# Pacing the side work of a hybrid encoder layer: Fourier tables split once, two paces, one more high part

## The chip, the cores and the metric

The kernel runs on one core of one Trainium2 chip, in one launch. The metric is the device time of that launch in microseconds (us). Before the change it is 2509.24 us, the median of three runs (2506.54 to 2513.37).

## The reference

One layer over T = 2048 positions of 1024 channels (a batch of one), all in float32:

```python
h = rms_norm(x, norm_g)
z = h @ w_in                                   # 1024 x 10240 columns
a_val, qkv, c_in, d_in, br_gates, merge = split(z)
y_a = real(fft2(a_val in 4 groups of 128 channels, over (positions, channels)))
y_b = neighborhood_attention(q, k, v, rpb)     # 8 heads, 32 x 64 grid, 8 x 16 window
y_c = silu(layer_norm(depthwise_conv31(ga * sigmoid(gb))))
y_d = u * (w_s @ layer_norm(v) + b)            # per chunk of 128 positions
proj   = [ (y_n * silu(gate_n)) @ w_branch[n] for n in 4 branches ]     # 512 -> 1024
merged = sum(sigmoid(merge_n) * proj_n)
out    = rms_norm(x + merged @ w_out, final_g)
```

## The kernel before

Each float32 operand is split in two parts of a reduced matmul type: a high part, cast on ScalarE (`split`, L226), and a low part, the difference, on VectorE (L227). A product is three matmuls, high by high, high by low and low by high (`mm3`, L235 to L244). The positions are worked in two halves of 1024.

**The first phase** (here: z phase) computes z = h @ w_in in 20 blocks of 512 columns per half, in the order of `BLOCKS` (L32 to L37): mixers and gates first, and as the last eight, blocks 12 to 19, the merge gates m3, n3, m2, n2, m0, n0, m1, n1. A block is done as seven products after Strassen and Winograd (`ORDER`, L53), 168 matmuls of 128x512. The weights come in tiles `wq` on SyncE's queue (SP) and are split into `whi` and `wlo`, five in advance (`W_BUFS`).

**Sides.** What is not the large products is written as Python generators ("sides"), which `tick` (L172) advances between the matmuls. A tick follows 6 matmuls, so that a block has 28; at each tick a side gains as many steps as its rate says. A side that must have ended by a certain block is drained there: all of its remaining steps are emitted at once. The rates and the blocks thus set where each instruction is written in the program; Tile, which builds the program, then sets each engine's order with the written order as priority. Each engine runs its own list in that order and waits by semaphores. The sides of the second half in question are:

- `conv_norm` (L826): the layer norm of the convolution in five pieces of 208 positions: channel sums (POOL adds at L230, a matmul at L802, VectorE at L849, ScalarE squares at L852, a second sum), then a square root (L859), reciprocals (L867), products (L871), 20 Silu activations (L875) and the stores. Its rate is `NORM_RATE`. It is drained at block `F_AT` = 15.
- `fourier` (L1081), begun at the same block, in four channel groups. Each group loads 1 MB (`fa`), does the butterflies on VectorE (L1109 to L1162), splits the result into `XS` (L226, L227), and then in `sums` (L1177) does products with nine tables (48 matmuls of 256 columns) and with a cosine and a sine (18 of 384). The tables `t_fft` are loaded as `traw` and split into `tH` and `tL` anew in each group. One rate, `FFT_RATE`, goes for all of it. It is drained at block 19.

**The second phase** (y phase) goes, for each half, through the branches 3, 2, 0, 1 and then the output product. Per branch, `project` (L1384) runs 8 column tiles (`dt`) of four `mm3` each (`kt`) on the four parts `yH`, `yL`. These parts come from `gated` (L1368): a part's `yL` is loaded, cast into `yH` (one of `YH_BUFS` = 5 buffers) and subtracted. Branch 1 (attention) has a gate besides, loaded into the only buffer `bg` and multiplied on VectorE. `ahead` (L1299) places the next branch's parts: part 0 at dt 6, and parts 1, 2 and 3 at dt 7, behind kt 0, 2 and 3. The branch's four parts in use hold four of the five buffers.

Beside the y phase runs the side `attention` (L941) with 128 items of 128 queries each: scores on PE (L997) and a minimum on VectorE (L1003); exp (L1006) and a scaling (L1008) on ScalarE; `turn`, four transposes on PE (L1019) and a split (L1021, L1022); `apply`, the products with v (L1035, L1037). `ATT_TURN` = 2 is the number of scores by which an item's transposes stand behind its own scores, `SC_BUFS` = 4 the buffers for scores, and `ATT_RATE` = (1.45, 0.85) the steps per tick, the second number in the branch-1 block of half 0. `fetch` (L1292) emits what steps are missing there before it loads the attention's result as a part of branch 1.

Of the kernel before, what the change touches and what calls it, by code (L numbers as in the profile page):

```python
# [9 lines left out]
F32 = mybir.dt.float32  # L10
F32R = mybir.dt.float32r
BF16 = mybir.dt.bfloat16
# [5 lines left out]
P = 128  # L18
# [37 lines left out]
CTYPE = (0, 1, 1, 2)  # L56

CONV_RATE = (0.55, 0.72)
NORM_RATE = (1.3, 1.6)
MIX_RATE = 0.7  # L60
FFT_RATE = 2.1
ATT_RATE = (1.45, 0.85)

X_AT = 17
F_AT = 15

Z_BUFS = 3
ZS_BUFS = 4
W_BUFS = 5
YH_BUFS = 5  # L70
YL_BUFS = 6
YW_BUFS = 4
SG_BUFS = 2
SC_BUFS = 4
VT_BUFS = 4

ATT_LEAD = 8
ATT_TURN = 2
ATT_APPLY = 3
FFT_LEAD = 12  # L80
SUM_LEAD = 4
# [3 lines left out]
PRE_RATE = 0.24  # L85
# [78 lines left out]
class Trunk:  # L164
# [254 lines left out]
    def scratch(self):  # L419
        d = lambda n, s, t=F32: self.dp.tile(s, t, name=n, tag=n)  # L420
        self.qd = [d(f"qd{j}", [2, P, T], F32R) for j in range(4)]
        self.kd = [d(f"kd{j}", [2, P, T], F32R) for j in range(4)]

        self.vd = d("vd", [8, GW, 4, ROWS // 4, P], F32R)
        self.fd = d("fd", [P, 16, W])
        self.yd = [[d(f"yd{n}{c}", [P, T]) for c in range(4)] for n in range(4)]
        self.gd = [[d(f"gd{n}{c}", [P, T]) for c in range(4)] for n in range(3)]

        self.wbd = [[d(f"wb{n}{i}", [P, 2, 512], F32R) for i in range(KT)] for n in range(4)]
        self.wod = [[d(f"wo{u}{i}", [P, 2, 512], F32R) for i in range(KT)] for u in range(2)]  # L430
        self.md = [[[d(f"md{n}{c}{h}", [P, HALF]) for h in range(2)] for c in range(KT)] for n in range(4)]
# [89 lines left out]
    def z_phase(self, ctx):  # L521
# [25 lines left out]
        for i in range(4):  # L547
            self.w_load(0, i)
        self.x_load(0, range(4, 8))
        xl, mix, conv, fft, pre = (self.side(r) for r in (2.0, MIX_RATE, CONV_RATE[0], FFT_RATE, PRE_RATE))  # L550
        self.conv, self.glu = conv, {}
        self.conv_side = self.sides[2]
        ps = [(self.psz if k < 2 else self.psp)() for k in range(4)]
        for j in range(4):
            self.x_square(j)
# [526 lines left out]
    def fourier(self):  # L1082
        nc, pool = self.nc, self.fp
        for _ in range(FFT_LEAD):
            yield
        raw = self.zs().rearrange("p (a c) -> p a c", a=4)[:, 0:2]
        self.load(out=raw, in_=self.io["t_cs"].rearrange("p (a c) -> p a c", a=2))
        cH = pool.tile([P, 2, P], F32R, name="cH", tag="cH")
        cL = pool.tile([P, 2, P], F32R, name="cL", tag="cL")
        self.split(cH, cL, raw)  # L1090
        self.cH, self.cL = cH, cL
        for g in range(4):
            yield from self.butterflies(g)
            yield from self.sums(g, *self.fX)

    def butterflies(self, g):
# [72 lines left out]
    def sums(self, g, XH, XL):  # L1169
        nc, pool = self.nc, self.fp  # L1170
        tt = nc.vector.tensor_tensor
        A, S = ALU.add, ALU.subtract
        cH, cL = self.cH, self.cL
        yt = pool.tile([P, T], F32, name="yf", tag="f8", bufs=3)
        yv = yt.rearrange("p (k1 k2) -> p k2 k1", k2=16)

        raws, ahead = [], []  # L1177

        def table(k):
            if k < 9:  # L1180
                raw = pool.tile([P, 3 * P], F32, name="traw", tag="traw", bufs=2)
                self.load(out=raw, in_=self.io["t_fft"][:, k * 384:(k + 1) * 384])
                raws.append(raw)

        def parts(k):
            if k < 9:
                tH = pool.tile([P, 3 * P], F32R, name="tH", tag="tH", bufs=2)
                tL = pool.tile([P, 3 * P], F32R, name="tL", tag="tL", bufs=2)
                self.split(tH, tL, raws.pop(0))
                ahead.append((tH, tL))  # L1190
                table(k + 2)

        table(0)
        table(1)
# [3 lines left out]
        for k0, k9 in ((0, 3), (3, 6), (6, 9)):  # L1198
            n = k9 - k0

            fH = pool.tile([P, 2, 3, P], F32R, name="fH", tag="fH")
            fL = pool.tile([P, 2, 3, P], F32R, name="fL", tag="fL")
            for k in range(k0, k9):
                yield
                tH, tL = ahead.pop(0)
                parts(k + 1)
                yield
                o = self.psp()[:, 0:2 * P]
                cplx = 0 < k < 8
                self.mm3([o], (XH[:, k], XL[:, k]), [(tH[:, P:3 * P], tL[:, P:3 * P])], True, not cplx)  # L1210
                if cplx:
                    self.mm3([o], (XH[:, 8 + k], XL[:, 8 + k]), [(tH[:, 0:2 * P], tL[:, 0:2 * P])], False, True)
                src = o.rearrange("p (s c) -> p s c", s=2)
                fh = fH[:, :, k - k0]
                nc.scalar.copy(fh, src)
                tt(out=fL[:, :, k - k0], in0=src, in1=fh.bitcast(F32), op=S)
            for _ in range(3):
                yield

            pu, pv = self.psp()[:, :n * P], self.psp()[:, :n * P]  # L1220
            for o, i in ((pu, 0), (pv, 1)):
                self.mm3([o], (cH[:, i], cL[:, i]),
                         [tuple(f[:, i, 0:n].rearrange("p k c -> p (k c)") for f in (fH, fL))], True, True)
            vs = self.zs()
            nc.scalar.copy(vs[:, :n * P], pv)
            pu3 = pu.rearrange("p (k c) -> p k c", c=P)
            vs3 = vs[:, :n * P].rearrange("p (k c) -> p k c", c=P)
            tt(out=yv[:, k0:k9], in0=pu3, in1=vs3, op=S)
            lo, hi = max(k0, 1), min(k9, 8)
            if lo < hi:  # L1230

# [33 lines left out]
    def y_phase(self, ctx):  # L1265
# [18 lines left out]
        for bi, (half, n) in enumerate(blocks):  # L1284
# [15 lines left out]
            def ahead(dt, kt):  # L1300

                if following is None or bi % 4 == 3:
                    return
                if dt == 4 and kt < 2:
                    fetch(kt)
                elif dt == 6 and kt == 0:
                    self.gated(nxt, *following, 0)
                elif dt == 7:
                    if kt < 2:
                        fetch(kt + 2)  # L1310
                    self.gated(nxt, *following, (1, None, 2, 3)[kt])

            self.project(ys, mg, bi % 4 == 0, ahead)
            if bi == 0:
# [52 lines left out]

    def gated(self, ys, half, n, kt):  # L1368

        if kt is None:  # L1370
            return
# [70 lines left out]
    def finish(self, u, row, ss, ps, t0):  # L1442
        nc, pool = self.nc, self.bp
        o = row[u]
        self.tt(o, ps, o, ALU.add)
        junk = pool.tile([P, 512], BF16, name="junk", tag="junk", bufs=1)
        nc.scalar.activation(out=junk, in_=o, func=AF.Square, accum_out=ss[:, u:u + 1])
        self.tt(o, o, self.fgb[:, 512 * u:512 * u + 512], ALU.mult, None if u else nc.gpsimd)
        if u == 0:
# [25 lines left out]
```

## Time and profile before

| | |
|---|---|
| median of three runs | 2509.24 us |
| the profiled execution | 2512.59 us |
| its span, first to last instruction | 2510.8 us (1.8 us lie around it) |
| mean granted TensorE clock | 0.982 |
| PE busy | 2398.4 us, 96% |
| VectorE (DVE), ScalarE (ACT), POOL busy | 1711.0, 1221.4, 337.4 us |
| DMA | 516.23 MB, 206 GB/s over the span |
| blocks 12 to 19 of the second half, start to end | 1339.4 to 1722.0 us |
| y phase, half 0 / half 1 | 1723.6 to 2188.7 / 2188.7 to 2510.8 us |

PE is the engine that is nearly always busy. A microsecond in which PE stands idle in the midst of the span, or runs below its full clock, can be won; work on any other engine costs only where PE, or a store at the end, waits for it. In the second half, blocks 14 to 19 start at 1417.6, 1457.7, 1522.6, 1581.9, 1631.7 and 1683.8 us.

### The profile page before, as it was taken

What the parts mean: (1) busy time and instruction counts of PE and PEld (TensorE: products, weight loads), DVE (VectorE), ACT (ScalarE), POOL (GpSimd) and SP (SyncE); (2) the same over time, 40 slices, a digit from 0 to 9 for tenths busy, and PEclk for the clock granted to TensorE, in tenths of its full rate; (3) what the DMA queues carried; (4) which work ended last, traced back from release to release, by engine and by line L of the source; (5) the groups of instructions that cost most, each with busy time, mean ns of one, the idle gap of its engine ahead of it and who ended that gap; (6) DMA issues with size and microseconds to landing.
All of it is one profiled execution on the core that took longest, in us unless ns stands there. A gap on an engine that the chain in (4) does not pass through costs nothing.

```text
span 2510.8 us, 34022 instructions
## 1 busy us (share of the span) xinstructions
PE 2398.4 (96%) x11804; PEld 1999.8 (80%) x11804; DVE 1711.0 (68%) x2972; ACT 1221.4 (49%) x2282; POOL 337.4 (13%) x290
## 2 busy tenths in 40 slices
PE   7999999999999999999999978999999799999998
PEld 6998878878878899877878867887777588777786
DVE  7585799996565537479898367764677776565433
ACT  5343545544574534354544565543655646652012
POOL 1000000000221100000000220001244333312220
PEclk9999999999999999999999989999999899999999
DMA  4353766654565335376755456667899788876566
GB/s 162 127 157 137 258 220 224 221 178 168 180 240 185 118 119 150 130 234 212 243 185 167 140 183 204 222 213 242 259 275 274 223 268 264 290 270 226 208 234 216
DMA packets 251720, 516.23 MB, mean 206 GB/s; under 512 B 26006, under 2 KB 124054, under 8 KB 250908
## 3 DMA queue, kind: packets, MB, share of 16 engines
q1 hardware_dynamic: 197276, 442.73, 54.7%
q10 hardware_dynamic: 54272, 71.32, 8.0%
q8 instruction: 93, 1.52, 0.2%
q14 instruction: 79, 0.65, 0.1%
HBM read 346.18 MB, written 167.77 MB: 205 GB/s over the span
## 4 chain that ended last, share of the span: by engine, by line
PE 64%; DVE 17%; DMA 8%; ACT 5%; issue 5%; POOL 1%; SPq 0%; ACTq 0%; DVEq 0%; POOLq 0%
PE z L238 36%; PE b L238 17%; DVE acc L785 6%; PE p L238 3%; DVE wlo L227 2%; PE p L1019 2%; PE p L997 2%; DMA pw<-in_wb_dram 2%; PE p L1035 1%; PE p L503 1%; DMA pw<-in_wo_dram 1%; DVE wq L230 1%; ACT sc L1006 1%; DMA yd<-yf 1%; DVE zu L233 1%
## 5 line engine op out<-in xcount | busy, mean ns | idle before, releaser
L226 ACT CAST whi<-wq 128x512 fp32r<-128x512 f32 x560 | 347.0, 621 | 489.4 <-PE z L238 282.1
L227 DVE TENSOR_TENSOR wlo<-wq,whi 128x512 fp32r<-128x512 f32 x560 | 391.7, 702 | 263.8 <-ACT whi L226 254.1
L238 PE MATMUL z<-hH,whi 128*128 128x512 f32 x1088 | 428.1, 394 | 10.5 <-ACT whi L226 8.0
L238 PE MATMUL z<-hH,wlo 128*128 128x512 f32 x1088 | 425.3, 391 | 1.6 <-DVE wlo L227 1.6
L238 PE MATMUL z<-hL,whi 128*128 128x512 f32 x1088 | 424.8, 390 | 0.0
L238 PE MATMUL b<-hH,whi 128*128 128x512 f32 x816 | 323.7, 397 | 8.5 <-DVE zu L233 8.3
L238 PE MATMUL z<-yH,yw 128*128 128x512 f32 x1024 | 308.7, 404 | 17.1 <-ACT yH L226 12.8
L238 PE MATMUL b<-hH,wlo 128*128 128x512 f32 x816 | 320.1, 392 | 0.8 <-DVE wlo L227 0.8
L238 PE MATMUL b<-hL,whi 128*128 128x512 f32 x816 | 320.2, 392 | 0.0
L785 DVE SCALAR_TENSOR_TENSOR acc<-hb,cw,acc 128x1009 f32<-128x1009 f32 (+1 forms) x240 | 306.7, 1281 | 2.0 <-ACT acc L781 1.5
L238 PEld LDWEIGHTS z<-hH,whi 128*128 128x128 f32 x1088 | 205.2, 189 | 54.9 <-ACT whi L226 8.5
L238 PEld LDWEIGHTS z<-yH,yw 128*128 128x128 f32 x1024 | 192.9, 193 | 61.5 <-ACT yH L226 17.5
L238 PEld LDWEIGHTS z<-hH,wlo 128*128 128x128 f32 x1088 | 204.9, 188 | 45.5 <-DVE wlo L227 2.3
L238 PEld LDWEIGHTS z<-hL,whi 128*128 128x128 f32 x1088 | 205.1, 188 | 41.1
L984 POOL TENSOR_TENSOR e<-mask,gt 128x512 f32<-128x512 bf16 x96 | 133.0, 1414 | 448.4 <-DMA gt<-in_rp_dram 380.9
L238 PEld LDWEIGHTS b<-hH,whi 128*128 128x128 f32 x816 | 154.4, 189 | 45.1 <-DVE zu L233 11.4
L238 PEld LDWEIGHTS b<-hH,wlo 128*128 128x128 f32 x816 | 154.5, 189 | 33.2 <-DVE wlo L227 1.1
L238 PEld LDWEIGHTS b<-hL,whi 128*128 128x128 f32 x816 | 154.4, 189 | 29.8
L238 PE MATMUL z<-yL,yw 128*128 128x512 f32 x512 | 164.9, 399 | 2.8 <-DVE yL L227 2.8
L1006 ACT ACTIVATE sc<-sc,mn 128x512 f32<-128x512 f32 x128 | 92.1, 720 | 97.4 <-DVE mn L1003 97.2
L1022 DVE TENSOR_TENSOR pp<-p,pp 128x512 fp32r<-128x512 f32 x128 | 87.1, 685 | 55.6 <-ACT pp L1021 55.3
L238 PE MATMUL z<-yw,mH 128*128 128x512 f32 x384 | 121.3, 397 | 2.6 <-DMA yw<-wo 2.1
(232 smaller groups left out, 4195.6 us busy)
## 6 DMA issues: line engine op xcount, KB each, us to landing
wq<-in_wz_dram SPq DMA_DIRECT2D x140, 512.0 KB, 3.6
wk<-wq SPq DMA_DIRECT2D x80, 512.0 KB, 2.7
wq<-wk SPq DMA_DIRECT2D x80, 512.0 KB, 3.9
yw<-wb SPq DMA_DIRECT2D x64, 512.0 KB, 4.6
sg<-md SPq DMA_DIRECT2D x64, 512.0 KB, 4.9
yw<-wo SPq DMA_DIRECT2D x64, 512.0 KB, 4.3
vt<-vd SPq DMA_DIRECT2D x64, 320.0 KB, 7.3
md<-zs ACTq DMA_DIRECT2D x64, 256.0 KB, 3.3
```

The lines of the kernel that those rows point to most:

```text
L226: nc.scalar.copy(hi, src)
L227: (eng or nc.vector).tensor_tensor(out=lo, in0=src, in1=hi.bitcast(F32), op=ALU.subtract)
L230: (eng or self.nc.vector).tensor_tensor(out=out, in0=a, in1=b, op=op)
L233: self.nc.vector.tensor_tensor(out=out, in0=a, in1=b, op=ALU.add)
L238: mm = lambda *a, **kw: self.nc.tensor.matmul(*a, skip_group_check=chained, **kw)
L503: self.nc.tensor.transpose(ps[:, j * P:(j + 1) * P], self.x_parts(j, which)[:, k * P:(k + 1) * P], self.ident)
L785: nc.vector.scalar_tensor_tensor(out=a, in0=hb[:, j:j + n], scalar=self.cw[:, i, j:j + 1], in1=a, op0=ALU.mult, op1=ALU.add)
L984: nc.gpsimd.tensor_tensor(out=ev, in0=mv, in1=gv, op=ALU.subtract)
L997: nc.tensor.matmul(ps, qs[:, i, 3 - cw, P - P * ri:2 * P - P * ri], ks[:, ri:ri + 4, 4 * c0:4 * c0 + P], start=i == 0, stop=i == 1)
L1006: nc.scalar.activation(out=s2, in_=s2, func=AF.Exp, scale=-1.0, bias=mn[:, 0:1], accum_out=sm)
L1019: nc.tensor.transpose(pt[:, b * P:(b + 1) * P], pr[:, b * P:(b + 1) * P], self.ident)
L1022: nc.vector.tensor_tensor(out=pl[:, ri], in0=pt, in1=ph[:, ri].bitcast(F32), op=ALU.subtract)
```

## The change

Seven constants change; the Fourier side gets one pace for the butterflies and another for the sums; the tables are split in group 0 only, stored in DRAM with both parts (`td`, nine of 384 KB) and loaded whole (`tf`, three buffers) in groups 1 to 3; the parts 0 and 1 of the next branch are made at dt 5; and the output's scratch tile `junk` takes the buffer of `bg`.

```diff
-NORM_RATE = (1.3, 1.6)
+NORM_RATE = (1.3, 2.0)
-FFT_RATE = 2.1
-ATT_RATE = (1.45, 0.85)
+FFT_RATE = (1.15, 2.3)
+ATT_RATE = (1.6, 0.74)
-F_AT = 15
+F_AT = 14
-YH_BUFS = 5
+YH_BUFS = 6
-SC_BUFS = 4
+SC_BUFS = 5
-ATT_TURN = 2
+ATT_TURN = 3
...
         for g in range(4):
+            self.fft_side[1] = FFT_RATE[0]
             yield from self.butterflies(g)
+            self.fft_side[1] = FFT_RATE[1]
             yield from self.sums(g, *self.fX)
...
         def table(k):
             if k < 9:
-                raw = pool.tile([P, 3 * P], F32, name="traw", tag="traw", bufs=2)
-                self.load(out=raw, in_=self.io["t_fft"][:, k * 384:(k + 1) * 384])
-                raws.append(raw)
+                t = pool.tile([P, 2, 3 * P], F32R, name="tf", tag="tf", bufs=3)
+                if g == 0:
+                    raws.append(self.zs()[:, 0:3 * P])
+                    self.load(raws[-1], self.io["t_fft"][:, k * 384:(k + 1) * 384])
+                else:
+                    self.load(t.rearrange("p s x -> p (s x)"), self.td[k].rearrange("p s x -> p (s x)"))
+                ahead.append(t)
         def parts(k):
-            if k < 9:
-                tH = pool.tile([P, 3 * P], F32R, name="tH", tag="tH", bufs=2)
-                tL = pool.tile([P, 3 * P], F32R, name="tL", tag="tL", bufs=2)
-                self.split(tH, tL, raws.pop(0))
-                ahead.append((tH, tL))
-                table(k + 2)
+            if k < 9 and g == 0:
+                t = ahead[0]
+                self.split(t[:, 0], t[:, 1], raws.pop(0))
+                self.store(self.td[k].rearrange("p s x -> p (s x)"), t.rearrange("p s x -> p (s x)"))
...
-                elif dt == 6 and kt == 0:
-                    self.gated(nxt, *following, 0)
+                elif dt == 5 and kt % 2 == 0:
+                    self.gated(nxt, *following, kt // 2)
                 elif dt == 7:
                     if kt < 2:
                         fetch(kt + 2)
-                    self.gated(nxt, *following, (1, None, 2, 3)[kt])
+                    else:
+                        self.gated(nxt, *following, kt)
...
-        junk = pool.tile([P, 512], BF16, name="junk", tag="junk", bufs=1)
+        junk = pool.tile([P, 512], F32, name="junk", tag="bg", bufs=1)
```

Three places show how the written order moves. The first is ScalarE's list at the end of `conv_norm` in the second half. Before, at the start of block 15, the first of its Silu pieces and the last sixteen stand ahead of the next weight cast; `acc` is the convolution, `b` a partial product of the block.

```order
L875 ACT_TABLE_LOAD
L875 ACTIVATE acc<-acc,cvec 128x208
L219 DMA md_185<-zs 128x512
L875 ACTIVATE acc<-acc,cvec 128x208 x15
L226 CAST whi<-wq_13612 128x512
L374 COPY b<-z 128x512
```

In the changed program (one line number higher), at the start of block 14, it reads:

```order
L708 ACTIVATE zs<-z 128x512
L226 CAST whi<-wq_13329 128x512
L219 DMA md_188<-zs 128x512
L708 ACTIVATE zs<-z 128x512
L876 ACT_TABLE_LOAD
L876 ACTIVATE acc<-acc,cvec 128x207 x4
L876 ACTIVATE acc<-acc,cvec 128x208 x12
L219 DMA md_192<-zs 128x512
L876 ACTIVATE acc<-acc,cvec 128x208 x4
L226 CAST whi<-wq_13388 128x512
L381 COPY zu<-z 128x512
```

The tail moved one block forward, and all twenty Silus stand in one row there, ahead of the casts of the tile wq_13388.

The second is SP's list of loads in the second Fourier group; `td` is the stored table, `wk` a weight sum kept in DRAM. Before:

```order
L210 DMA wq_14580<-in_wz_dram 128x1024
L210 DMA wq_14668<-wk 128x1024
L210 DMA traw<-in_t_fft_dram 128x384 x2
L210 DMA wq_14752<-wk 128x1024
L210 DMA traw<-in_t_fft_dram 128x384 x4
L210 DMA wq_14838<-wk 128x1024
L210 DMA traw<-in_t_fft_dram 128x384
```

In the changed program the same place reads:

```order
L210 DMA tf<-td_101 128x768
L210 DMA tf<-td_102 128x768
L210 DMA wq_14540<-in_wz_dram 128x1024
L210 DMA tf<-td_103 128x768
L210 DMA wq_14620<-in_wz_dram 128x1024
L210 DMA tf<-td_104 128x768
L210 DMA tf<-td_105 128x768
L210 DMA tf<-td_106 128x768
L210 DMA wq_14701<-in_wz_dram 128x1024
```

Loads of twice the size stand among the weight loads, up to three in a row.

The third is PE's list at the start of the branch-1 block of half 0. Before, `sc_18812` is transposed directly behind the second scores that follow it, and the block's own products come in with the last rows:

```order
L997 MATMUL p_18853<-ks_18516,qs_18515 128x512 x2
L1019 MATMUL p_18864<-t_ident_229,sc_18764 128x128 x4
L997 MATMUL p_18871<-ks_18516,qs_18515 128x512 x2
L1019 MATMUL p_18881<-t_ident_229,sc_18812 128x128 x4
L238 MATMUL z_19053<-yH_18657,yw_18412 128x512
L238 MATMUL z_19054<-yH_18657,yw_18412 128x512
L1035 MATMUL p_18888<-pp_18795,vt_18605 128x512 x3
L1037 MATMUL p_18888<-pp_18795,vt_18605 128x2x128 x2
L997 MATMUL p_18901<-ks_18516,qs_18515 128x512 x2
```

In the changed program:

```order
L1020 MATMUL p_19052<-t_ident_238,sc_18895 128x128 x4
L998 MATMUL p_19077<-ks_18644,qs_18643 128x512 x2
L1020 MATMUL p_19093<-t_ident_238,sc_18936 128x128 x4
L1036 MATMUL p_19100<-pp_18943,vt_18739 128x512 x3
L1038 MATMUL p_19100<-pp_18943,vt_18739 128x2x128 x2
L998 MATMUL p_19123<-ks_18644,qs_18643 128x512 x2
L1020 MATMUL p_19150<-t_ident_238,sc_18982 128x128 x4
L998 MATMUL p_19171<-ks_18644,qs_18643 128x512 x2
L1020 MATMUL p_19193<-t_ident_238,sc_19032 128x128 x4
```

Each set of transposes now has three sets of scores, not two, between its own scores and itself.

## Rows read from the trace of the kernel before

**Rows 1.** The page's first part: busy time, share of the span, instructions.

```profile
PE 2398.4 (96%) x11804; PEld 1999.8 (80%) x11804; DVE 1711.0 (68%) x2972; ACT 1221.4 (49%) x2282; POOL 337.4 (13%) x290
```

**Rows 2.** By stretch: length, busy time of each engine, clock, DMA share, GB/s.

```profile
100.00:150.00 50.00, 50.00 (x419) 50.00 (x419) 33.15 (x63) 18.79 (x35) 0.00 (x0) 1.00 0.39 127
1339.40:1377.60 38.20, 38.20 (x170) 31.62 (x170) 33.03 (x36) 17.51 (x30) 1.60 (x2) 1.00 0.46 151
1457.70:1522.60 64.90, 49.14 (x221) 40.17 (x220) 43.58 (x97) 37.83 (x74) 13.04 (x20) 0.89 0.60 184
1522.60:1581.90 59.30, 51.57 (x249) 43.31 (x248) 43.57 (x95) 29.16 (x61) 0.00 (x0) 0.94 0.63 202
1581.90:1631.70 49.80, 47.56 (x236) 40.07 (x235) 39.38 (x88) 26.58 (x54) 0.00 (x0) 1.00 0.69 227
1631.70:1683.80 52.10, 49.36 (x236) 41.38 (x235) 40.12 (x88) 25.61 (x52) 0.00 (x0) 0.97 0.57 196
```

**Rows 3.** PE's waits, 1457.7 to 1722 us: total, times, longest.

```profile
PE p L238 <- ACT XS L226: 19.1, 4, 7.5
PE z L238 <- ACT whi L226: 8.0, 1, 8.0
```

**Rows 4.** Timeline at block 15's start: start, us, engine, line, [idle before].

```profile
1463.45 7.34 ACT L875 ACTIVATE acc<-acc,cvec 128x208 f32<-128x208 f32 x16
1471.35 1.28 PE L238 MATMUL z<-hH,whi 128*128 128x512 f32 x2 [8.03 <-ACT whi L226]
```

**Rows 5.** By line: total busy us, mean ns; first three 1380 to 1480, last whole.

```profile
L230 POOL TENSOR_TENSOR cn<-cn 128x208 f32<-128x208 f32 (+1 forms) x19 | 13.6, 727 | 56.3 <-ACT cn L852 55.9
L849 DVE SCALAR_TENSOR_TENSOR acc<-p,acc 128x208 f32<-128x208 f32 (+1 forms) x20 | 6.2, 367 | 3.7 <-PE p L802 3.7
L867 DVE RECIPROCAL rs<-rs 128x208 f32<-128x208 f32 (+1 forms) x5 | 7.0, 1428 | 0.4 <-ACT rs L859 0.4
...
L875 ACT ACT_TABLE_LOAD x5 | 6.4, 1283 | 0.4 <-ACT whi L226 0.3
```

**Rows 6.** Timeline of the second Fourier group, VectorE and PE.

```profile
1541.88 1.22 DVE L1111 TENSOR_TENSOR fs<-fa 128x1024 f32<-128x1024 f32 x1
...
1553.13 0.58 PE L238 MATMUL p<-tH,XS 128*128 128x256 f32 x1 [7.55 <-ACT XS L226]
```

**Rows 7.** By line over the whole span: the table splits.

```profile
L227 DVE TENSOR_TENSOR tL<-traw,tH 128x384 fp32r<-128x384 f32 x36 | 20.0, 554 | 9.7 <-ACT tH L226 9.5
L226 ACT CAST tH<-traw 128x384 fp32r<-128x384 f32 x36 | 18.5, 514 | 14.8 <-DMA traw<-in_t_fft_dram 12.9 <-DVE wlo L227 1.7
```

**Rows 8.** DMA issues: count, KB each, median us to landing.

```profile
wq<-in_wz_dram SPq DMA_DIRECT2D x140, 512.0 KB, 3.6
zs<-gd SPq DMA_DIRECT2D x16, 256.0 KB, 4.1
```

**Rows 9.** By stretch: the y phase to its last block, branch 2 of half 0, a burst.

```profile
1723.60:2412.00 688.40, 645.23 (x3009) 518.46 (x3010) 439.71 (x988) 346.73 (x687) 217.08 (x151) 0.97 0.79 250
...
1793.60:1878.90 85.30, 80.23 (x398) 64.56 (x396) 63.17 (x158) 54.76 (x112) 28.31 (x21) 0.98 0.91 264
...
1968.90:2012.00 43.10, 34.07 (x140) 25.49 (x138) 29.73 (x73) 28.41 (x59) 16.15 (x12) 0.79 0.74 201
```

**Rows 10.** PE's waits, 1723 to 2412 us.

```profile
PE z L238 <- ACT yH L226: 12.8, 8, 3.1
PE p L1019 <- ACT sc L1008: 7.7, 5, 2.8
PE p L997 <- DVE pp L1022: 5.1, 5, 2.4
```

**Rows 11.** By line, ScalarE alone, 1723 to 2250 us.

```profile
L1006 ACT ACTIVATE sc<-sc,mn 128x512 f32<-128x512 f32 x122 | 87.7, 719 | 89.3 <-DVE mn L1003 89.1
```

**Rows 12.** Timeline at the start of the branch-1 block of half 1.

```profile
2364.09 1.22 DVE L230 TENSOR_TENSOR bg<-yL,bg 128x1024 f32<-128x1024 f32 x1 [4.39 <-DMA bg<-gd]
2366.52 2.07 PE L238 MATMUL z<-yH,yw 128*128 128x512 f32 x4 [3.14 <-ACT yH L226]
```

More of the change, by code (lines that the diff above doesn't have):

```diff
@@ L427, in scratch @@
         self.gd = [[d(f"gd{n}{c}", [P, T]) for c in range(4)] for n in range(3)]
+        self.td = [d(f"td{i}", [P, 2, 3 * P], F32R) for i in range(9)]
         self.wbd = [[d(f"wb{n}{i}", [P, 2, 512], F32R) for i in range(KT)] for n in range(4)]
@@ L549, in z_phase @@
         self.x_load(0, range(4, 8))
-        xl, mix, conv, fft, pre = (self.side(r) for r in (2.0, MIX_RATE, CONV_RATE[0], FFT_RATE, PRE_RATE))
+        xl, mix, conv, fft, pre = (self.side(r) for r in (2.0, MIX_RATE, CONV_RATE[0], FFT_RATE[0], PRE_RATE))
         self.conv, self.glu = conv, {}
-        self.conv_side = self.sides[2]
+        self.conv_side, self.fft_side = self.sides[2:4]
         ps = [(self.psz if k < 2 else self.psp)() for k in range(4)]
@@ L1085, in fourier @@
             yield
+        cs = pool.tile([P, 2, 2, P], F32R, name="cs", tag="cs")
         raw = self.zs().rearrange("p (a c) -> p a c", a=4)[:, 0:2]
         self.load(out=raw, in_=self.io["t_cs"].rearrange("p (a c) -> p a c", a=2))
[L1088 to L1091, printed above, removed]
+        self.split(cs[:, 0], cs[:, 1], raw)
+        self.cH, self.cL = cs[:, 0], cs[:, 1]
         for g in range(4):
+            self.fft_side[1] = FFT_RATE[0]
             yield from self.butterflies(g)
+            self.fft_side[1] = FFT_RATE[1]
             yield from self.sums(g, *self.fX)
@@ L1175, in sums @@
         yv = yt.rearrange("p (k1 k2) -> p k2 k1", k2=16)
-        raws, ahead = [], []
+        ahead, raws = [], []
         def table(k):
             if k < 9:
-                raw = pool.tile([P, 3 * P], F32, name="traw", tag="traw", bufs=2)
-                self.load(out=raw, in_=self.io["t_fft"][:, k * 384:(k + 1) * 384])
-                raws.append(raw)
-        def parts(k):
-            if k < 9:
-                tH = pool.tile([P, 3 * P], F32R, name="tH", tag="tH", bufs=2)
-                tL = pool.tile([P, 3 * P], F32R, name="tL", tag="tL", bufs=2)
-                self.split(tH, tL, raws.pop(0))
-                ahead.append((tH, tL))
-                table(k + 2)
+                t = pool.tile([P, 2, 3 * P], F32R, name="tf", tag="tf", bufs=3)
[5 more added lines that the diff above has]
+                ahead.append(t)
+        def parts(k):
+            if k < 9 and g == 0:
+                t = ahead[0]
+                self.split(t[:, 0], t[:, 1], raws.pop(0))
+                self.store(self.td[k].rearrange("p s x -> p (s x)"), t.rearrange("p s x -> p (s x)"))
         table(0)
@@ L1204, in sums @@
                 yield
-                tH, tL = ahead.pop(0)
+                t = ahead.pop(0)
+                tH, tL = t[:, 0], t[:, 1]
                 parts(k + 1)
+                table(k + 2)
                 yield
@@ L1368, in gated @@
     def gated(self, ys, half, n, kt):
-        if kt is None:
-            return
         nc, pool = self.nc, self.bp
```

## The prediction

> **What bounds the kernel now.** The page's busy shares come first: PE works 2398.4 us of a span of 2510.8 [rows 1], and no other engine comes near, so I look only for stretches in which PE stands or its clock is low. The stretches by block show where. An undisturbed block of 168 large matmuls takes 38.2 us, .2274 each [rows 2]. Blocks 15 to 18 of the second half take 64.9 + 59.3 + 49.8 + 52.1 = 226.1 us [rows 2]. They hold four such blocks (152.8) and the Fourier products: 192 matmuls of 256 columns at .119 (419 in a fully busy 50 us [rows 2]), 22.9, and 72 of 384 columns at three quarters of .2274, 12.3. That is 188.0, so 38.1 us are lost. PE's waits name three quarters of it: 19.1 us at four places for the split butterflies `XS`, the longest 7.5, and 8.0 us at one place for a weight cast [rows 3]. The timeline shows the latter: sixteen Silus of the layer norm, 7.34 us, run on ScalarE directly ahead of the cast [rows 4]. The third part is the clock. It was granted at .89, .94 and .97 in three of these blocks; the lost share of their busy time is .11 x 49.1 + .06 x 51.6 + .03 x 49.4 = 10.0 us [rows 2]. All three stretches hold the waits, and the undisturbed block has 1.00: the clock falls where PE has stood.
>
> The y phase up to its last block has 688.4 - 645.2 = 43.2 us without PE work, and at a mean clock of .97 another .03 x 645 = 19 [rows 9]. The worst place is the start of the branch-1 block of half 0: in 43.1 us PE works 34.1 at clock .79, while ScalarE and VectorE each work 28 to 30 us [rows 9]. Attention items come back to back there, because steps not done by then are forced. By cause, 12.8 us are waits of the first products for `yH`, 7.7 of transposes for the scaled scores, 5.1 of scores for a PSUM buffer that a split still reads [rows 10].
>
> **The change part by part.**
>
> *The layer norm's tail* moves from block 15 to block 14 and is paced faster. Nothing of it is saved. In the new order PE has 69 large matmuls between the last channel sum and the first product that needs a cast from behind the twenty Silus: 69 x .2274 = 15.7 us of cover. ScalarE's list in that time holds three table loads at 1.28 [rows 5], the root and a few casts, some 7 us, and then 20 Silus at .46 (7.34 / 16 [rows 4]), 9.2. VectorE, which feeds the Silus, has five reciprocals at 1.43 [rows 5] and 20 products at about the .37 of the like operation [rows 5], 14.5 us. Either chain ends some 17 to 19 us after the sum, so about 3 us are waited for. Ahead of that three channel sums stand closely behind one another in PE's list, 14, 1 and 12 matmuls apart; each waits for POOL adds of .73, three of them in two levels, and squares [rows 5], and I put 1.7, .9 and 1.6 there. That is 7 against 8.0 before: **-1**. From below, no wait at all would be -8, with 2 of clock -10. From above, all three sums bare (each about 3.6 for adds and squares, together 11) and 15 us of Silu chain without cover give 26, or +18. I stay at the nearest row, the 8.0.
>
> The Trainium skill, ScalarE: Activation LUTs, section "Table sets: the hidden batching unit", says that a change between function sets costs a table load of about 2.7 us, so that activations should be batched by set; here a root and two Silu stretches follow one another on the path. With its figure the three loads would make 8.1 instead of 3.8, and the tail would wait 4 us more. The row shows 1.283 for one load; I keep to the row.
>
> *The butterflies' own pace.* Before, the time on PE's list between the first butterfly and the first product that reads it, summed with the durations of these rows over the order, is 10.7, 15.0, 17.5 and 17.7 us for the four groups; VectorE's list holds 12.8, 16.5, 17.1 and 17.1 us up to the first `XS`. In the second group the chain runs from 1541.88 to 1553.13 and PE waits 7.55 of it [rows 6]. After, PE has 10.9, 11.3, 23.6 and 22.9, VectorE 12.8, 13.5, 20.1 and 18.9. The last two groups are thus covered by 3.5 and 4.0 us, and their waits, 19.1 less the two longest of 7.3 and 7.5, 4.3 us together, go. The first two keep about the shortfall that the first had before; since a block is now spread over more work between the groups, I take 2 us off each. Sum **-8** of the 19.1 [rows 3]; bounds 0, when the scheduler's order gives the cover back elsewhere, and -19.
>
> *The clock in these blocks* follows the waits: of 10.0 us I take **-4**, in proportion (8 of 19); bounds 0 and -10.
>
> *The tables.* 27 of 36 splits go: 27 x .554 on VectorE and 27 x .514 on ScalarE [rows 7], 15.0 and 13.9 us. PE waits for neither (they are not among its waits [rows 3]), so they are worth nothing by themselves: **0**. For them come 9 stores and 27 loads of 384 KB on SP's in-order queue, in place of 27 loads of 192 KB. A weight load of 512 KB lands in 3.6 us, a load of 256 KB in 4.1 [rows 8]; so I put one at about 4. From issue to use PE's list holds 4.7 to 8.5 us of work in the three groups (three buffers allow two loads ahead). It holds if nothing is in front. The upper bound is the slower rival below, +46.
>
> The Trainium skill, DMA: Bandwidth & Descriptors, section "Anatomy of one DMA — SWDGE (gpsimd) path", gives a fixed 2.0 us and the bytes at 436 GB/s: an estimate of 2.9 us for 384 KB. By that every table would land in time; the rows here, on another kind of queue, show a smaller load taking 4.1, so the margin is thinner than the page makes it.
>
> *The y phase.* (a) Attention's rate goes from 1.45 to 1.6 in the earlier blocks. By the order, 148 steps are then written where 146 are needed; before, ten were missing and forced into the start of the branch-1 block, which now holds 14 items instead of 18 (the three blocks before it 18, 26 and 27 instead of 17, 24 and 25). The burst costs 9.0 us of idle time and .21 x 34.1 = 7.2 of clock [rows 9]; with a quarter fewer items and none of them forced I take -7. What pays is the earlier blocks: one more exp and scaling of .72 each [rows 11] per 15 us, on a ScalarE that is busy 55 of 85 us [rows 9]; that is covered. (b) Parts 0 and 1 are made at dt 5, some 15 us before the block ends, with a sixth buffer. At the last branch-1 block the single `bg` was loaded late (4.39 us waited), and PE waited 3.14 and again about 2 [rows 12]; with its clock this goes, -5. (c) A third score between an item's score and its transposes gives 1.35 us more of PE work (the four scores, transposes and products of an item, by the order) against a chain of 2 x .72 [rows 11]: of 7.7 + 5.1 [rows 10] I take -3. Sum **-15**; bounds +5 (two more items per block make waits like those of now) and -30 (half of 43 + 19).
>
> *The rest.* `junk` in the buffer of `bg` lies in the output product, where `bg` is not needed: 0. The cosine table's merge: 0.
>
> **Sum.** -1 - 8 - 4 + 0 - 15 = -28 us on the profiled execution: 2512.6 - 28 = 2484.6. That execution stood 3.4 above the median, so 2481.2: forecast **2481**. Its own range is 2466 to 2496.
>
> **Rivals.**
> - *Only the y phase gains.* The waits for `XS` are moved, not removed: the first two groups stay as short of cover as before (10.9 against 12.8), and the tail in block 14 costs what the last two groups win. For it speaks that the largest two waits are exactly these; against it the 23 us of cover of the last two. Then 2509.2 - 15 = 2494.
> - *Nearly all goes.* -4 for the tail, -17 `XS`, -9 clock, -28 y phase: 2451. For it speaks that waits and low clock come together in each stretch; against it that the order leaves two groups short and that 14 items stay in the burst's block.
> - *Next to nothing.* The waits of the y phase turn out to be VectorE's and ScalarE's own throughput in the attention items, which does not change; the moved pieces wait elsewhere. Then about -4: 2505.
> - *Slower: the tables on SP.* SP issues in order, and a weight load that waits for its buffer holds up the table loads written behind it; then each of the 27 tables lands after the load in front: 3.6 + 4.1 = 7.7 us [rows 8] against a mean cover of 6, 1.7 us late, 46 us in all. With the gains of -28 that is +18 on the forecast's basis: 2527. It decides from a landing later than the cover, 4.7 us in the tightest cases. For it speaks the new order, with up to three table loads in a row behind a weight load; against it a DMA share of only .60 to .69 in these blocks [rows 2], when the y phase runs at .91 with PE 94% busy [rows 9], and less work on both engines that free the weight buffers.
>
> **Chances.** Forecast .50, only the y phase .18, nearly all .13, next to nothing .09, slower .10. About 0.3% (7.5 us) is what a measurement of this kernel tells from no change: faster means below 2501.7, slower above 2516.8. Faster: .50 + .13 + nearly all of .18 (.16) + .01 of the .09 = .80; the same: .02 + .08 = .10; slower .10. The range reaches from the middle of the second rival, 2451, to beyond the fourth, 2508; outside it lie the slower case and half of the fastest, .17.
>
> **What would show it.** In the profile after: PE's waits between block 14 and 19 for `XS` drop to about 11 us, in the first two groups alone; the wait for `whi` behind the Silus is about 3 us long and lies in block 14, with shorter ones for the channel sums; no wait of PE for `tf`; the clock in the Fourier blocks .95 and more; the start of the branch-1 block of half 0 runs above .85; that of half 1 has no wait above 1 us for `yH`. I am wrong if `tf` loads appear among PE's waits, if the tail in block 14 costs above 15 us, or if the scores' waits in the three blocks of half 0 grow by more than the burst loses.

## The result and the profile after

The changed kernel takes 2475.33 us (median of four runs, 2474.92 to 2476.64), against 2511.3 for the kernel before (median of four, 2506.54 to 2518.12): the ratio of the two is 0.9856, with a 95% interval of 0.9831 to 0.988. That is 36 us less; 28 were forecast. Its profiled execution took 2475.09 us with a span of 2473.3. One execution of one run below, e12_turn_two, took 4743.82 us where its other three took 2486.68 to 2490.06; the ratios leave it out.

The page's first part for the changed kernel, to be held against [rows 1]:

```profile
PE 2384.8 (96%) x11804; PEld 1987.8 (80%) x11804; DVE 1699.2 (69%) x2945; ACT 1205.7 (49%) x2251; POOL 341.7 (14%) x290
```

PE has the same 11804 matmuls. Its idle time went from 112 to 88 us, and its busy time fell by 14, since the same matmuls ran at a higher granted clock, .993 in the mean against .982.

The stretches of the changed kernel, with the columns of [rows 2]: block 14, block 15, blocks 14 to 18 together, the whole stretch from the y phase's start, and the parts of it that stand in [rows 9].

```profile
1422.30:1474.30 52.00, 44.31 (x177) 34.49 (x176) 31.57 (x54) 35.95 (x67) 19.67 (x29) 0.93 0.66 200
1474.30:1527.00 52.70, 48.77 (x235) 39.50 (x234) 41.22 (x91) 25.79 (x52) 0.00 (x0) 1.00 0.84 295
...
1422.30:1671.00 248.70, 235.12 (x1113) 195.03 (x1112) 172.27 (x369) 130.06 (x250) 19.67 (x29) 0.99 0.73 246
...
1709.10:2473.30 764.20, 725.41 (x3392) 583.86 (x3392) 469.93 (x1048) 370.31 (x745) 233.46 (x160) 0.99 0.80 255
...
1709.10:2376.60 667.50, 637.97 (x3009) 512.04 (x3010) 440.89 (x989) 346.33 (x689) 221.75 (x151) 0.99 0.82 258
1957.00:2000.00 43.00, 33.84 (x139) 24.44 (x138) 33.69 (x72) 24.87 (x49) 15.31 (x10) 0.88 0.80 253
```

The same two stretches of the kernel before, cut at the same places of the program:

```profile
1417.60:1683.80 266.20, 237.72 (x1116) 198.25 (x1115) 184.78 (x396) 143.08 (x280) 22.49 (x34) 0.96 0.60 195
...
1722.00:2510.80 788.80, 734.35 (x3392) 591.31 (x3392) 469.79 (x1048) 373.43 (x747) 229.66 (x160) 0.97 0.77 247
```

Blocks 14 to 18 are 17.5 us shorter: idle 28.5 to 13.6, and 2.6 from the clock. The y phase with the output is 24.6 shorter: 15.7 of idle time, 8.9 of busy time. The sum is 42; block 14 began 4.7 us later than before. A run below that leaves the norm, the Fourier side and the tables as before (e1_y_only) began it at 1422.2 too, and over all the profiled runs below it began between 1421.6 and 1429.2. So nothing ties those 4.7 us to the change; what they are stays open.

PE's waits in the changed kernel, 1422 to 1709 us, the four largest, against [rows 3]:

```profile
PE b L238 <- DVE zu L233: 5.3, 3, 2.3
PE b L238 <- DVE wlo L227: 2.9, 1, 2.9
PE p L803 <- POOL cn L230: 2.8, 3, 1.4
PE p L238 <- ACT XS L226: 1.5, 2, 0.8
```

The waits for `XS` fell from 19.1 to 1.5 us, all of them and not only those of the last two groups. No load of a table is waited for; the two waits that are left out are for a copied partial product, 0.5 us, and for a split table in the first group, 0.3. The layer norm's tail is still there, in pieces: the channel sums 2.8, and 2.9 for a low part `wlo` that stands in VectorE's list behind the reciprocals and products for the Silus. It is not the cast behind the Silus on ScalarE that is waited for, as it was before.

The first Fourier group before, from SP's, VectorE's and PE's timelines (start, us, engine, line, idle before):

```profile
1484.40 0.58 SPq L210 DMA_DIRECT2D fa<-fd  x1
1491.49 1.23 DVE L1109 TENSOR_TENSOR fs<-fa 128x1024 f32<-128x1024 f32 x1 [4.04 <-DMA fa<-fd]
1502.48 0.80 PE L238 MATMUL p<-tH,XS 128*128 128x256 f32 x2 [7.28 <-ACT XS L226]
```

The same in the changed kernel:

```profile
1466.10 0.58 SPq L210 DMA_DIRECT2D fa<-fd  x1
1474.65 1.23 DVE L1111 TENSOR_TENSOR fs<-fa 128x1024 f32<-128x1024 f32 x1 [2.02 <-DMA fa<-fd]
1485.63 0.86 PE L238 MATMUL p<-tf,XS 128*128 128x256 f32 x5 [0.78 <-ACT XS L226]
```

From the first butterfly to the first product it is 11.0 us in both. But the chain begins with a load of 1 MB that is issued 7 to 8.5 us earlier still. From its issue to the product the chain takes 18 to 20 us in the two kernels and in three of the experiments below; what differs is how much work PE has in that time (e4_old_pace has the old paces and the old block, e3_one_pace and e7_even_pace one pace from block 14).

| first group | issue to product, us | PE busy in it (matmuls) | PE's wait for `XS` at its end |
|---|---|---|---|
| before | 18.1 | 10.8 (49) | 7.3 |
| e4_old_pace | 17.7 | 10.9 (49) | 6.8 |
| e3_one_pace | 19.0 | 15.8 (60) | 2.0 |
| e7_even_pace | 19.8 | 15.8 (60) | 2.0 |
| change | 19.5 | 17.4 (67) | 0.8 |

Cover is to be counted from the load. Most of what was won here comes with the earlier block; the slow pace adds the rest.

In the second group the chain itself was broken before: VectorE's timeline between its first two butterflies.

```profile
1534.02 1.23 DVE L1109 TENSOR_TENSOR fs<-fa 128x1024 f32<-128x1024 f32 x1 [2.06 <-DMA fa<-fd]
...
1538.75 0.69 DVE L230 TENSOR_TENSOR yf<-yf,zs 128x512 f32<-128x512 f32 x1 [1.52 <-DMA zs<-gd]
1540.67 0.69 DVE L230 TENSOR_TENSOR yf<-yf,zs 128x512 f32<-128x512 f32 x1 [1.23 <-DMA zs<-gd]
...
1541.88 1.22 DVE L1111 TENSOR_TENSOR fs<-fa 128x1024 f32<-128x1024 f32 x1
```

The gate products of the group before, with their own loads, stood between, 6.6 us. In the changed kernel all four end ahead of the first butterfly, and the second follows it directly. The runs below bear this out: with 5.8 us between the two butterflies PE waits 6.4 in this group (e1), with 5.7 it waits 5.2 (e7), with 2.2 it waits 0.9 (e3), with 1.1 it waits 0.4 (e4).

The new loads among the DMA rows of the changed kernel, as in [rows 8]:

```profile
tf<-td SPq DMA_DIRECT2D x27, 384.0 KB, 4.0
```

PE's waits of the changed kernel from 1709 to 2377 us, the y phase to its last block, the three largest, against [rows 10]:

```profile
PE z L238 <- ACT yH L226: 6.8, 6, 2.0
PE p L998 <- DMA qs<-qd: 3.8, 1, 3.8
PE p L1020 <- DVE mn L1004: 3.6, 6, 0.9
```

The waits for the scaled scores, 7.7 before, are gone from it, those for `yH` fell from 12.8 to 6.8, and one for a load of q is new.

### The profile page after: what moved, and what is told of

It reads as the page before. It is cut to its first block, busy times and chain, and to the rows that moved or that the text cites. A ratio compares the mean times of both kernels' runs of the same rounds, so it can differ in the third digit from the quotient of the medians.

```text
span 2473.3 us, 34008 instructions
## 1 busy us (share of the span) xinstructions
PE 2384.8 (96%) x11804; PEld 1987.8 (80%) x11804; DVE 1699.2 (69%) x2945; ACT 1205.7 (49%) x2251; POOL 341.7 (14%) x290
## 5 line engine op out<-in xcount | busy, mean ns | idle before, releaser
L238 PE MATMUL b<-hH,whi 128*128 128x512 f32 x816 | 323.4, 396 | 16.1 <-DVE zu L233 15.9
L238 PEld LDWEIGHTS b<-hH,whi 128*128 128x128 f32 x816 | 153.8, 188 | 54.7 <-DVE zu L233 16.1
L1004 DVE CUSTOM_DVE_ANT_0 sc<-p,e 128x512 f32<-128x512 f32 x128 | 87.1, 684 | 58.0 <-PE p L998 38.7
```

The costliest lines, as they stand in the source:

```text
L238: mm = lambda *a, **kw: self.nc.tensor.matmul(*a, skip_group_check=chained, **kw)
L1004: nc.vector.tensor_tensor_reduce(out=s2, in0=ps, in1=e, scale=1.0, scalar=3.0e38, op0=ALU.add, op1=ALU.min, accum_out=mn)
```

## The experiments

Each ratio is against the kernel before, run beside the run in question (its medians there are 2512.05 to 2515.57). The lengths are from the profile, between the first products: blocks 14 to 18, and the y phase with the output. How far a length may be read is seen where the code of a stretch is the change's: blocks 14 to 18 then take 247.5 to 250.1 us (e5, e6, e8, e10, e12), the y phase 764.5 to 770.0 (e1 to e4, e7, e9, e11).

| run | ratio (95% interval) | median us | blocks 14 to 18 | y phase |
|---|---|---|---|---|
| before | 1 | 2511.3 | 266.2 | 788.8 |
| change | 0.9856 (0.9831 to 0.988) | 2475.33 | 248.7 | 764.2 |
| e1_y_only | 0.9926 (0.9911 to 0.9941) | 2494.7 | 265.1 | 764.5 |
| e2_tables_back | 0.9867 (0.985 to 0.9883) | 2480.96 | 249.3 | 766.0 |
| e3_one_pace | 0.9958 (0.9943 to 0.9972) | 2503.85 | 274.3 | 765.8 |
| e4_old_pace | 0.9928 (0.9913 to 0.9943) | 2495.07 | 266.8 | 765.0 |
| e5_parts_late | 0.993 (0.9908 to 0.9952) | 2495.65 | 248.5 | 780.3 |
| e6_att_back | 0.9943 (0.9927 to 0.996) | 2497.54 | 248.4 | 783.2 |
| e7_even_pace | 0.9953 (0.9938 to 0.9967) | 2500.19 | 268.2 | 767.1 |
| e8_bg_pool | 0.9922 (0.9905 to 0.994) | 2492.44 | 248.4 | 781.0 |
| e9_norm28 | 0.9884 (0.9865 to 0.9904) | 2485.25 | 245.9 | 770.0 |
| e10_att_fast | 0.9949 (0.993 to 0.9967) | 2501.72 | 250.1 | 789.3 |
| e11_fft_slow | 0.9871 (0.9854 to 0.9888) | 2481.6 | 253.1 | 768.4 |
| e12_turn_two | 0.9891 (0.9862 to 0.9919) | 2489.84 | 247.5 | 780.5 |

**The two halves.** The kernel before with the y phase's edits alone (`ATT_RATE`, `YH_BUFS`, `SC_BUFS`, `ATT_TURN`, the parts at dt 5, `junk`).

> The kernel before, with the edits of the y phase alone (attention's paces, six high parts at dt 5, transposes three scores behind, five score buffers); norm, Fourier paces and tables as before. Theory (the two halves of the change add up; the y phase of the changed kernel is 24.6 us shorter by the blocks' starts): 2486, between 2482 and 2490. Rival (the two phases are coupled: the y phase gains because the z phase ends with less left over): 2495 or more.

The y phase is 764.5 us, as in the change, and blocks 14 to 18 are as before. The halves add up: no coupling. The time, 2494.7 or 18.7 us below its own reference of 2513.36, lies outside the 2482 to 2490. In its profiled execution (2491.77 us) block 14 again began 4.6 us later than in the profile of before; the rest of the miss stays open.

**The tables.**

```diff
...
-                t = pool.tile([P, 2, 3 * P], F32R, name="tf", tag="tf", bufs=3)
...
+                raw = pool.tile([P, 3 * P], F32, name="traw", tag="traw", bufs=2)
...
+                self.split(tH, tL, raws.pop(0))
...
```

> The changed kernel, but the tables are loaded and split anew in each of the four groups. Theory (the splits lie beside PE's work and are worth nothing by themselves; the pace removed the waits for XS): 2475, within 3 us, and waits of PE for XS below 4 us in all. Rival (the 29 us of splits taken off VectorE and ScalarE are what let the butterflies end in time): XS waits of 8 us and more come back, 2484 or more.

Blocks 14 to 18 take 249.3 us and PE waits 1.6 for `XS`: 27 splits more cost 0.6 us, though VectorE is busy 13 us more there. The stored tables are worth nothing measurable; the intervals of the two ratios overlap. The median is 3 us above what was expected; in the profile block 14 begins 6.9 us later than in the change.

**The paces.** In the changed kernel, one pace:

```diff
-FFT_RATE = (1.15, 2.3)
+FFT_RATE = (2.1, 2.1)
```

> The changed kernel with one Fourier pace of 2.1 for butterflies and sums, begun at block 14 as in the change. Theory (the slow pace of the butterflies gives them cover): the waits for XS come back with 12 to 19 us, and the clock with them, 2488 to 2497. Rival (the earlier start and the tables removed them, not the pace): XS waits below 5 us, within 4 us of 2475.

and in another, all the old paces:

```diff
-NORM_RATE = (1.3, 2.0)
+NORM_RATE = (1.3, 1.6)
...
-FFT_RATE = (1.15, 2.3)
+FFT_RATE = (2.1, 2.1)
...
-F_AT = 14
+F_AT = 15
```

> The changed kernel with all paces of the z phase as before (norm 1.6, Fourier 2.1 from block 15): of the z phase only the tables are changed. Theory (tables worth nothing): waits for XS near 19 us and the 8 us behind the Silus are back, 2490 to 2496. Rival (the tables carry the gain of the z phase): 2480 or less, XS waits below 6 us.

With the old paces and the old block the whole gain of the z phase is gone (266.8): PE waits 14.2 us for `XS` and again 8.0 for the cast behind the Silus. With block 14 and one pace it is worse than before, 274.3, and the time lies above both theories. The waits for `XS` came back only in part, 7.4 us for the high and 0.9 for the low part, not the 12 to 19 expected; the clock takes more, as the stretch of that run shows:

```profile
1423.70:1698.00 274.30, 247.66 (x1112) 204.89 (x1112) 172.18 (x369) 129.60 (x250) 19.79 (x29) 0.94 0.72 244
```

Its PE busy time is 12.5 us above the change's with the same matmuls, at a clock of .94 against .99; its idle time is 26.6 against 13.6, in many short waits. Its block 15 alone takes 77.9 us at a clock of .87 and holds 301 matmuls, where the change's takes 52.7 at 1.00 with 235: the old pace packs the products close behind the butterflies. The third run of this kind has one pace too, but ends after as many ticks as the change's two:

```diff
-FFT_RATE = (1.15, 2.3)
+FFT_RATE = (1.78, 1.78)
```

> The changed kernel with one Fourier pace of 1.78, which ends after as many ticks as the two paces do. Theory (the slow butterflies give the cover, not the five blocks over which the work is spread): XS waits of 7 us and more, blocks 14 to 18 longer by 6 to 15 us, 2481 to 2490. Rival (it is the spreading): XS waits below 3 us, within 4 us of 2475.

It takes 268.2, 19.5 more than the change (6 to 15 were expected), and the time lies 10 us above the theory's range. PE's waits over blocks 14 to 18 of this run:

```profile
PE p L238 <- ACT XS L226: 11.0, 4, 5.2
...
PE p L238 <- DVE XS L227: 2.6, 2, 1.5
```

So with the block and the tables of the change, two paces instead of one are worth 19.5 to 25.6 us; neither the earlier block alone nor the longer spread gives the gain. By groups, PE's waits for `XS` (both parts) are:

| run | group 1 | group 2 | group 3 | group 4 |
|---|---|---|---|---|
| before | 7.3 | 7.6 | 2.2 | 2.0 |
| e4_old_pace | 6.8 | 0.4 | 4.2 | 2.8 |
| e3_one_pace | 2.9 | 0.9 | 2.5 | 1.9 |
| e7_even_pace | 3.1 | 5.2 | 3.4 | 2.0 |
| change | 0.8 | 0.8 | 0 | 0 |

The two paces clear groups 3 and 4, which no run with one pace does. In group 1 the earlier block takes off most of the wait, and group 2 hangs on the gate products. No run changes only one of the two paces, and none has the two paces from block 15, so what the earlier block adds to them, and which of the two numbers does more, is not shown.

A pace slower still, with quicker sums, changes nothing for the better:

```diff
-FFT_RATE = (1.15, 2.3)
+FFT_RATE = (1.0, 2.6)
```

> The changed kernel with Fourier paces of 1.0 for the butterflies and 2.6 for the sums, which end after about as many ticks. Theory (the butterflies' cover is enough at 1.15, XS waits are 1.5 us already; quicker sums bring ScalarE's and VectorE's part of a product closer to the next use): blocks 14 to 18 within 2 us of the 248.5 of the change, or up to 5 longer, 2475 to 2480. Rival (more cover is still worth something in the first two groups): 2471 or less.

Blocks 14 to 18 are 253.1, 4.4 longer, with `XS` waits of 1.9: the cover is enough at 1.15. The time lies 1.6 us above the range.

**The norm's tail.**

```diff
-NORM_RATE = (1.3, 2.0)
+NORM_RATE = (1.3, 2.8)
```

> The changed kernel with a layer norm pace of 2.8 instead of 2.0 in the second half. Theory (block 14 costs some 13 us more than its matmuls because 57 steps of the norm are drained at its start at once: three channel sums behind one another, then the root and twenty Silus ahead of a weight cast): with fewer steps left the waits of PE for the sums, 2.8 us, go, block 14 loses 3 to 6 us less, 2469 to 2473. Rival (the twenty Silus and their products set the end, whenever they begin): within 2 us of 2475.

PE's waits for the channel sums fall from 2.8 to 0.5 us. Block 14 is 5.5 us shorter, but block 13 is 2.9 and block 15 3.9 longer. Blocks 13 to 18 of that run:

```profile
1385.00:1674.50 289.50, 276.43 (x1294) 228.79 (x1293) 190.49 (x399) 150.52 (x293) 31.92 (x47) 0.99 0.70 232
```

and of the change:

```profile
1381.60:1671.00 289.40, 275.82 (x1294) 228.93 (x1293) 188.80 (x399) 151.01 (x293) 32.20 (x47) 0.99 0.69 232
```

Nothing is won: the rival is right on the work, though its time was missed by 8 us. Of the 9.4 us between the two spans, 3.4 lie ahead of block 13 and 5.8 in a y phase whose edits are the change's; both stay unexplained.

**Parts and transposes.** First the parts, as before:

```diff
-YH_BUFS = 6
+YH_BUFS = 5
...
-                elif dt == 5 and kt % 2 == 0:
-                    self.gated(nxt, *following, kt // 2)
+                elif dt == 6 and kt == 0:
+                    self.gated(nxt, *following, 0)
...
```

> The changed kernel with five high parts and the next branch's parts made as before (part 0 at dt 6, the others at dt 7). Theory (the early parts are worth what the last branch-1 block won, 8 us, and 2 to 4 us at other block starts): 2484 to 2488, PE waits for yH near 12 us as before. Rival (attention's pace made those starts shorter, the parts don't matter): within 3 us of 2475.

The y phase is 16.1 us longer, and the time lies above both theories. PE's wait for `yH` is longer than either had it (from 1715 to 2400 us, where the change has 5.2):

```profile
PE z L238 <- ACT yH L226: 20.2, 10, 4.0
```

Then attention's three constants:

```diff
-ATT_RATE = (1.6, 0.74)
+ATT_RATE = (1.45, 0.85)
...
-SC_BUFS = 5
+SC_BUFS = 4
...
-ATT_TURN = 3
+ATT_TURN = 2
```

> The changed kernel with attention's paces (1.45, 0.85), four score buffers and transposes two scores behind, as before. Theory (attention's order gives the rest of the y phase's 24.6 us, that is what parts and buffers don't give): 2485 to 2492; the branch-1 block of half 0 is near 88 us again instead of 78. Rival (the block of 78 us only has fewer items, which others then hold: little is lost): 2479 or less.

The y phase is 19.0 us longer; the time lies 5.5 us above the theory's range. The branch-1 block of half 0 is nearly as long as before again. And two of the three, `SC_BUFS` = 4 and `ATT_TURN` = 2, with the new pace:

> The changed kernel with transposes two scores behind and four score buffers as before, but the new attention paces. Theory (of the 19 us that attention's order is worth, the third score is the larger part: with two, PE waits for ScalarE's scaled scores, 12.0 us in the run with all three constants back against 0.4): the y phase is 10 to 15 us longer, 2485 to 2490, score waits of 8 us and more. Rival (the pace is the larger part, since it takes the forced steps away): 2480 or less, score waits below 4 us.

The y phase is 16.3 us longer, a little more than the 10 to 15 expected, and transposes wait for the scaled scores as in no other run:

```profile
PE p L1020 <- ACT sc L1009: 14.7, 11, 3.0
```

By the y phase the third score with its fifth buffer is thus worth 16 of the 19. What is left for the pace, 3, is less than the 5.8 us by which y phases of equal code differ, so its worth isn't told from nothing here. The whole run shows less for the third score, a ratio of 0.9891 against 0.9856 (9 us), with intervals that overlap; the waits are the firmer evidence. The early parts' 16 and attention's 19 add to more than the whole 24.6: each of the two edits is worth more beside the other than alone. The sixth `yH` buffer and the earlier parts were taken back together, and so were the third score and its buffer; what each is worth by itself was not tested.

A still faster attention:

```diff
-ATT_RATE = (1.6, 0.74)
+ATT_RATE = (1.75, 0.74)
```

> The changed kernel with an attention pace of 1.75 instead of 1.6 in the first blocks of half 0. Theory (the start of the branch-1 block still waits for the last items that its parts need, and these end sooner): that block loses 4 to 8 us less than its 17, the blocks before it 2 to 3 us more, 2470 to 2474. Rival (VectorE and ScalarE, at 64 to 68 and 56 to 62 us of 86 to 90 us busy in branches 2 and 0, can't take more items): those blocks lose as much or more, 2475 to 2482.

It gives all 25 us back; the time lies 20 us above the rival's range. Branch 2 of half 0 takes 98.0 us instead of 86.4, and PE's largest wait in the y phase is for VectorE's minimum, 3.6 us in the change:

```profile
PE p L1020 <- DVE mn L1004: 9.8, 11, 1.7
```

The rival is right that a block ahead of the branch-1 block pays, but its size was missed.

**The load of q.** The changed kernel's burst at 1957 has its 3.8 us wait where SP's list holds, one behind the other,

```profile
1984.42 0.33 SPq L210 DMA_DIRECT2D bg<-gd  x1
1984.79 0.44 SPq L210 DMA_DIRECT2D ks<-kd  x1
1985.28 1.23 SPq L210 DMA_DIRECT2D qs<-qd  x2
```

and `bg` waited 11.3 us there for its buffer. Moved to GpSimd's queue:

```diff
-            self.load(gt, self.gd[n][kt][:, half * HALF:half * HALF + HALF])
+            self.load_q(gt, self.gd[n][kt][:, half * HALF:half * HALF + HALF])
```

> The changed kernel, but the gate of branch 1 (bg) is loaded by GpSimd's queue and no longer stands in SP's list, where it waits 11.3 us for its only buffer with the loads of q and k behind it. Theory (PE's wait of 3.8 us for q at the start of the branch-1 block of half 0, and a low clock after it, come from that): the wait goes, 2469 to 2473. Rival (GpSimd now waits instead and holds up the masks of attention): new waits of the scores for VectorE or GpSimd, 2475 or more.

The wait for q goes, and the y phase is 17 us longer; the scores now wait 10.1 us for VectorE, as the rival had it. GpSimd's, VectorE's and PE's timelines of that run, ahead of the branch-1 block:

```profile
1942.04 7.20 POOL L985 TENSOR_TENSOR e<-mask,gt 128x512 f32<-128x512 bf16 x4
1949.14 0.57 POOL L213 DMA_DIRECT2D bg<-gd  x1
...
1958.97 1.23 DVE L230 TENSOR_TENSOR bg<-yL,bg 128x1024 f32<-128x1024 f32 x1 [8.49 <-issue]
...
1960.19 0.67 DVE L1023 TENSOR_TENSOR pp<-p,pp 128x512 fp32r<-128x512 f32 x1
...
1960.92 1.22 PE L998 MATMUL p<-ks,qs 128*128 128x512 f32 x2 [7.88 <-DVE pp L1023]
```

The load is issued behind four masks, 3.6 us after its buffer came free (1945.5), and lands 9.8 us later; VectorE stands 8.5 us in front of the product with attention's pieces queued behind it. So the masks are not held up, as the rival thought, but hold up the load, and the greater part is the load's own time and the order on VectorE. A second buffer for `bg` was not tried.

No run here is faster than the change.

## Why the prediction was right, and where its terms were off

**The tail**, -1: right in size. The three sums wait 2.8 us (4.2 were put there), the chain behind the roots 2.9 (3), and 1.9 more for a sum of products in the same block: 7.6 against 7 and the 8.0 of [rows 3]. The wait at the chain's end is not the one for `whi` behind the Silus that was looked for; VectorE's reciprocals and products, the other of the two chains, hold up a low part. The table loads took 1.28 us each again, and ScalarE goes on directly: the load ahead of the Silus follows an activation that ends at 1439.25, and the first Silu starts at 1440.56. The 2.7 us of the Trainium skill (ScalarE: Activation LUTs, "Table sets: the hidden batching unit") are not borne out by any run here.

**The butterflies**, -8 of 19.1: mis-sized; -17.6 was measured. The step that failed is that "the first two keep about the shortfall that the first had before". I counted cover from the first butterfly on the written lists. By that count the first two groups were short by 2.1 and 1.5 us before, where PE waited 7.3 and 7.6, and the last two not at all, where it waited 2.2 and 2.0; so the count didn't hold even for the rows that it started from. The two rows of the first group show that the load of `fa` belongs to the chain, and the second group's that four gate products stood in it. In group 1 the earlier block gives PE 5 us more work behind the load's issue (15.8 in e3, which has one pace, against 10.8), and the slow pace 1.6 more. In group 2 the gate products end first. e3 and e7 show that the two paces are needed for the gain, e2 that the tables have no part.

**The clock**, -4: by the rows, lost busy time went from 10.0 us to .07 x 44.3 = 3.1, so -7, as most of the waits left; the four blocks behind block 14 ran at 1.00; block 14, which holds the tail, at .93. The matmuls show a smaller part of that, 2.6 us of busy time over all five blocks.

**The tables**, 0: right (0.6 us in e2). 4.0 us to landing was estimated at "about 4"; the tightest cover of 4.7 held, and the slower rival didn't come. Only where the sums were issued more densely did PE wait for a load of `tf` at all, 2.3 us in e3 and 0.8 in e4.

**The y phase**, -15: -24.6 was measured, and the parts differ from mine. (a) The burst didn't shrink by 7: [rows 9] had 34.1 of 43.1 us of work, now 33.8 of 43.0; only the clock rose, .79 to .88. The whole block got 10.1 us shorter, but by holding less work; its idle time is 9.2 us, where it was 9.6:

```profile
1968.90:2057.40 88.50, 78.95 (x353) 62.59 (x352) 62.95 (x142) 48.42 (x98) 35.27 (x25) 0.90 0.78 231
...
1957.00:2035.40 78.40, 69.24 (x305) 53.80 (x304) 57.36 (x118) 37.53 (x74) 31.43 (x21) 0.93 0.83 263
```

The first row is the kernel before, the second the change. No run shows the -7 that I put on the pace. (b) The early parts: -5 at the last branch-1 block was right in kind (the block went from 54.2 to 46.2 us, its waits for `yH` from 5.2 to 1.0), but e5 gives 16 us over all the block starts. (c) The third score was put at -3 and is worth 16 in e12's y phase, together with its buffer. The chain that I took, 2 x .72, left out its small steps. The changed kernel's ScalarE rows, 1709 to 2376 us:

```profile
L1007 ACT ACTIVATE sc<-sc,mn 128x512 f32<-128x512 f32 x128 | 92.5, 723 | 140.3 <-DVE mn L1004 140.2
L1009 ACT ACTIVATE sc<-sc,sm 128x512 f32<-128x512 f32 x128 | 90.6, 721 | 9.7 <-DVE sm L1008 9.4
L1007 ACT ACTIVATION_READ_ACCUMULATOR sc<-sc,mn 128x1 f32 x128 | 24.1, 188 | 0.0
```

With VectorE's minimum (.69 and .08 to read it) and reciprocal (.15), the chain is 2.55 us without a hand-over, against 2 x 1.35 = 2.7 of PE's work between two scores. That leaves 0.15 us for all the hand-overs. Over the 128 items of e12 the time from the minimum's start to the scaling's end is 2.5 us at the least and 3.05 in the median, so two scores don't cover it and three, 4.05, mostly do.

So the waits that were named are the ones that went, but the sum rests on terms that miss both ways: the butterflies, the early parts and the third score were costed low, the pace in the burst too high. By the stretches the change won 42 us, 14 more than forecast; the 4.7 us that block 14 began late, which nothing ties to the change, brought the measured 36 nearer to the 28. That part of the agreement is luck.

## What to carry to other kernels

Count the cover of a side chain from its first load's issue, and add every small instruction and every foreign one that stands in an engine's list between its links. A side that alternates between a long chain on one engine and dense products on another wants two paces; here an earlier start at one pace took most of the first wait away and still made the stretch 8 us longer than before (e3). Before a load is moved to another queue, look at what waits for it in order on the engine that uses it.

## What was not expected of the hardware

A stretch with many short waits also loses by its clock: with the same matmuls PE's busy time in blocks 14 to 18 was 235 us at a granted clock of .99 and 248 at .94 (e3). How the idle time is spread counts beside its sum: the kernel before stood 28.5 us in five kinds of waits, the longest 8.0, and was busy 238 at .96; e3 stood 26.6 in more and shorter ones. The 512 KB load that landed 9.8 us after GpSimd issued it was the slowest of eight, with a median of 4.9; from SP the row of the change has 4.5, and in [rows 12]'s block it was 5.8 (2358.33 to 2364.09). In the same 20 us of that run a load of 256 KB from SP took 9.4 and one of 512 KB 10.2, so loads from both queues were slow at that time, and no row here puts it on GpSimd's queue.
